# A two-part transformer on one core: wider token chunks, transform steps laid among attention steps, branch outputs kept in DRAM

## The chip, the core and the metric

The kernel runs on one core of a Trainium2 chip. The metric is the device time of one execution in microseconds (us). Engines: TensorE (PE) multiplies, VectorE (DVE) and ScalarE (ACT) do the element-wise work, GpSimd (POOL) a little, and SyncE (SP) issues all the DMAs from one queue, in order.

## The reference

Batch 1, 256 tokens, width 1024, all in fp32. The first part is a stack of two layers; each is a mixer, a cross-attention to 256 memory rows and a convolutional feed-forward net (FFN), with residual sums. The second part has two layers over a context stream and a token stream, which share weights:

```
x  = x + mixer(norm(x));  x = x + xattn(norm(x), norm(mem));  x = x + conv_ffn(norm(x))    # two layers
h  = modulate(x),  hc = modulate(xc);   proj = h @ w_in,  projc = hc @ w_in                # second part, two layers
o_mla  = attend(q_mla,  [k_mla_c,  k_mla_l],  [v_c, v_l])      # 8 heads, latent keys
o_gqa  = attend(q_gqa,  [k_gqa_c,  k_gqa_l],  [v_c, v_l])      # 8 heads, 2 key heads
o_four = real(fft over tokens and over the 128 columns of a group)   # 4 groups
y  = sig(g0)*(o_mla @ w0) + sig(g1)*(o_gqa @ w1) + sig(g2)*(o_four @ w2)
x  = x + gt1 * (y @ w_o);   x = x + gt2 * conv_ffn_2(modulate(x))
```

In the first of the second part's layers the context stream goes through all of this too; in the last layer only its keys and values are needed.

## The kernel before

**Products.** A weight matrix comes in units of 128 rows by up to 1024 columns. `Stream.unit` (L1501 and on) issues the DMA of one unit into a `raw` tile (five of them), ACT casts it to a high half (L106) and DVE takes the rest as a low half (L107); `hi` and `lo` have four buffers each. Each product is three fp32r matmuls, high by high, high by low and low by high: `mm3` (L127 to L129) has the weights stationary and gives features by tokens; `mm3t` (L133 to L135) has 128 tokens stationary and streams weight columns. `tok` calls `mm3t` chunk by chunk: normally 256 columns, both token halves in one PSUM bank; with `wide=True` 512 columns, a bank for each token half. Chunks of 512 columns were in use for the first half of each FFN's down product and in `mixer1`; all others were 256 wide.

**PSUM.** Eight banks: `mm` 2, `acc` 2, `at` 2 (logits), `tp` 1 (transposes), `ao` 1 (attention output). `use` says which of them the names A and B stand for.

**SBUF slots.** Activations of 2 KB a partition come from one pool of 25 slots, attention outputs, transform outputs, merge sums and their split halves among them.

**Order.** The program is written in an order by hand, and a planner then orders each engine's instructions by simulated time, with the written order as priority; a tile's buffer has to be free before its writer is placed. Independent work is written in as steps of generators: `fill` takes steps of the spare generator (the memory's keys and values, then the context stream's part of the second half), `tick` takes steps of the modulation product (L842 to L844). In the second part `layer2` walks the string `ORDER`: N norm of the tokens, K and V keys and values, G and Q queries, O one step of the grouped attention, A one of the latent attention (four each), F the whole transform, c, b and B steps of the context stream. After it `MERGE` says in which order the three gated branch sums (0 latent, 1 grouped, 2 transform) are written; each is a loop over 8 pairs of feature blocks.

**One attention step** (`attend`, L1166 and on) is, for two token halves: logits of two heads (L1178, into `at`), maximum on DVE (L1187), exponential on ACT (L1189), reciprocal and scaling on DVE (L1191, L1192), transposes (L1197, `tp`), copy on ACT (L1198), then weights times values (L1200, `ao`), and a copy to the slot `oa` (L1204).

**The transform** (`fourier`, L1208 and on) first loads three constants into `dr` tiles and splits them, once a layer. For each of 4 groups it then makes the features of all streams (`mm`), splits them, multiplies by the column transform (`acc`), splits, and multiplies by the token transform (`ao`).

## Time and profile before

| | us |
|---|---|
| median of 3 runs | 2317.23 (2313.97 to 2317.65) |
| the profiled execution's own time | 2314.78 |
| its span, first to last instruction | 2313.0 |
| PE busy | 2273.5 (98%) |
| DVE busy | 1510.2 (65%) |
| ACT busy | 1199.2 (52%) |
| DMA engines, mean busy share of the main queue | 48.1% |
| mean granted TensorE clock | 0.996 |

PE counts as busy while any matmul is under way. Matmuls overlap: one lasts longer than the step from its start to the next one's start, so a short wait between two can leave the busy time nearly whole. A row of the windows view has the stretch, its length, then for each engine its busy time and number of instructions (x) in the order PE, PEld (weight loads), DVE, ACT, POOL, then the granted clock (PEclk, 1.00 is 2.4 GHz), the busy share of the DMA engines and GB/s; for one line alone, only the engines that run it are there. In the timeline a row is start, duration, engine, line, operation, tiles and count. Stages by time: first layer 0 to 480 us, second layer 480 to 920, first layer of the second part 920 to 1820 (attention to 1140, merge sums to 1360, output and FFN after it), last layer 1820 to 2313 (attention to 2010).

### The profile page before, as it was taken

The numbers are of one execution on the slowest core, as the hardware profiler recorded it, in microseconds if no ns is written. First come the engines' busy times: TensorE is split into PE (matmuls) and PEld (weight loads), VectorE is DVE, ScalarE is ACT, GpSimd is POOL, SyncE is SP. The second block draws the span as 40 slices with busy tenths as digits, with TensorE's granted clock in tenths as the row PEclk, the third lists the DMA queues.
The fourth block names the chain that finished last, engine by engine and source line by source line (L and its number), as shares of the span: only waits on it lengthen the run. The fifth ranks groups of instructions, "written<-read, shape, count | busy, mean of one in ns | idle before, by whom it ended". The sixth has DMA issues, their size and how long they took to land.

```text
span 2313.0 us, 43514 instructions
## 1 busy us (share of the span) xinstructions
PE 2273.5 (98%) x17424; PEld 2104.5 (91%) x17424; DVE 1510.2 (65%) x2734; ACT 1199.2 (52%) x2220; POOL 106.6 (5%) x162
## 2 busy tenths in 40 slices
PE   8999999999999999899999999999999999999999
PEld 8899998988999999889899998789779989999999
DVE  6755586866757777776544446654566676677876
ACT  5655564654656555666433434331344566655554
POOL 2000000000001000121000000000000131000000
PEclk9999999999999999899999999999999999999999
DMA  8354576567446765323233244444444433375563
GB/s 274 122 171 147 180 245 220 172 199 264 130 133 215 236 195 177 114 65 102 65 120 121 92 164 147 155 157 130 166 158 142 144 115 128 102 243 177 173 201 128
DMA packets 114140, 369.29 MB, mean 160 GB/s; under 512 B 13432, under 2 KB 21505, under 8 KB 113937
## 3 DMA queue, kind: packets, MB, share of 16 engines
q1 hardware_dynamic: 113936, 366.50, 48.1%
q8 instruction: 137, 2.24, 0.4%
q14 instruction: 67, 0.54, 0.1%
HBM read 365.36 MB, written 1.09 MB: 158 GB/s over the span
## 4 chain that ended last, share of the span: by engine, by line
PE 94%; DVE 2%; ACT 2%; DMA 1%; issue 1%; POOL 0%; SPq 0%; POOLq 0%; ACTq 0%; DVEq 0%
PE mm L127 11%; PE mm L128 11%; PE mm L129 11%; PE acc L133 8%; PE acc L134 8%; PE acc L135 8%; PE acc L127 6%; PE acc L129 6%; PE acc L128 6%; PE at L1178 2%; PE ao L844 2%; PE mm L133 2%; PE mm L134 2%; PE mm L135 2%; PE ao L1200 2%; PE tp L1197 1%
## 5 line engine op out<-in xcount | busy, mean ns | idle before, releaser
L107 DVE TENSOR_TENSOR lo<-raw,hi 128x1024 fp32r<-128x1024 f32 (+4 forms) x615 | 709.6, 1158 | 447.9 <-ACT hi L106 437.9
L106 ACT CAST hi<-raw 128x1024 fp32r<-128x1024 f32 (+4 forms) x615 | 608.1, 994 | 666.5 <-PE mm L128 231.3
L127 PE MATMUL mm<-xt,hi 128*128 128x256 f32 (+1 forms) x1552 | 465.5, 300 | 2.1 <-ACT zq L961 2.0
L129 PE MATMUL mm<-xt,lo 128*128 128x256 f32 (+1 forms) x1552 | 461.4, 297 | 0.5 <-DVE lo L107 0.5
L128 PE MATMUL mm<-xt,hi 128*128 128x256 f32 x1376 | 391.7, 285 | 0.2 <-DVE xt L294 0.2
L127 PEld LDWEIGHTS mm<-xt,hi 128*128 128x128 f32 x1552 | 298.4, 192 | 22.3 <-issue 11.0
L129 PEld LDWEIGHTS mm<-xt,lo 128*128 128x128 f32 x1552 | 298.5, 192 | 8.6 <-DVE lo L107 1.1
L128 PEld LDWEIGHTS mm<-xt,hi 128*128 128x128 f32 x1376 | 265.4, 193 | 0.6 <-DVE xt L294 0.4
L129 PE MATMUL acc<-xt,lo 128*128 128x256 f32 (+1 forms) x704 | 218.4, 310 | 0.0
L127 PE MATMUL acc<-xt,hi 128*128 128x256 f32 (+1 forms) x704 | 217.9, 310 | 0.0
L128 PE MATMUL mm<-xc,hi 128*128 128x256 f32 (+1 forms) x544 | 174.1, 320 | 0.0
L128 PE MATMUL acc<-xt,hi 128*128 128x256 f32 x528 | 149.4, 283 | 0.0
L127 PEld LDWEIGHTS acc<-xt,hi 128*128 128x128 f32 x704 | 134.3, 191 | 7.8 <-issue 0.8
L129 PEld LDWEIGHTS acc<-xt,lo 128*128 128x128 f32 x704 | 134.3, 191 | 6.9
L133 PE MATMUL acc<-hi,wh 128*128 128x256 f32 x480 | 136.1, 285 | 0.0
L135 PE MATMUL acc<-hi,wl 128*128 128x256 f32 x480 | 135.8, 283 | 0.0
L134 PE MATMUL acc<-lo,wh 128*128 128x256 f32 x480 | 135.6, 283 | 0.0
L128 PEld LDWEIGHTS mm<-xc,hi 128*128 128x128 f32 x544 | 103.4, 190 | 7.7 <-DVE xc L294 0.3
L127 PE MATMUL mm<-xc,hi 128*128 128x256 f32 x368 | 105.1, 286 | 1.1 <-DVE xc L297 1.1
L129 PE MATMUL mm<-xc,lo 128*128 128x256 f32 x368 | 105.3, 286 | 0.0
L128 PEld LDWEIGHTS acc<-xt,hi 128*128 128x128 f32 x528 | 101.3, 192 | 0.1
L133 PEld LDWEIGHTS acc<-hi,wh 128*128 128x128 f32 x480 | 91.8, 192 | 3.0 <-issue 1.6
(489 smaller groups left out, 5167.1 us busy)
## 6 DMA issues: line engine op xcount, KB each, us to landing
raw<-in_w_up_dram SPq DMA_DIRECT2D x176, 512.0 KB, 3.6
raw<-in_w_mod_dram SPq DMA_DIRECT2D x96, 512.0 KB, 4.6
raw<-in_w_gb_dram SPq DMA_DIRECT2D x96, 512.0 KB, 3.6
raw<-in_w_dna_dram SPq DMA_DIRECT2D x30, 512.0 KB, 3.7
raw<-in_w_f_dram SPq DMA_DIRECT2D x25, 512.0 KB, 3.5
raw<-in_w_dnb_dram SPq DMA_DIRECT2D x24, 512.0 KB, 3.4
raw<-in_w_dn_dram SPq DMA_DIRECT2D x24, 512.0 KB, 3.7
raw<-in_w_qk_dram SPq DMA_DIRECT2D x16, 512.0 KB, 4.7
```

Source lines behind the costliest of these rows:

```text
L106: self.nc.scalar.copy(out=hi, in_=src)
L107: self.nc.vector.tensor_sub(out=lo, in0=src, in1=hi.bitcast(F32))
L127: m(ps, whi, xhi, start=first, stop=False)
L128: m(ps, whi, xlo, start=False, stop=False)
L129: m(ps, wlo, xhi, start=False, stop=last)
L133: m(ps, xhi, whi, start=first, stop=False)
L134: m(ps, xhi, wlo, start=False, stop=False)
L135: m(ps, xlo, whi, start=False, stop=last)
L844: nc.tensor.matmul(ps[32 * j:32 * j + 32, half * T:half * T + T], self.cs[:, k], raw[:, j], start=(k + half == 0), stop=(k + half == 8), t ...
L1178: lg = lambda u, i: nc.tensor.matmul(pss[i][:, u], qf(j, i, t), kf(j, i, u), start=True, stop=True)
L1197: nc.tensor.transpose(tp[:, u], es[(4 * g + u) // nk][:, u % nk], self.ident)
L1200: self.beside(nk, lambda u, i: nc.tensor.matmul(ops[64 * i:64 * i + 64, t], vf(j, i, u), pts[i][:, u], start=(u == 0), stop=(u == nk - 1)))
```

## The change

1. **512-column chunks.** The first two 256-column chunks become one of 512 in: the values of `mixer0` (chunks 2 and 3, `values2`), the four output projections of mixers and cross-attentions (`project`), the second half of both first-part FFNs, the second half of the second part's FFN for the context stream of its first layer and for the tokens of its last. The memory's values of layer 0 are two chunks of 512 instead of four of 256. They use the `mm` banks; their evictions handle one token half at a time.
2. **Orders.** The transform becomes a generator with one step a group, each merge sum one with 8 steps. In the first of the two layers the four F steps stand among the tokens' O and A steps; in the last layer they stand singly, and the 8 steps of branch sum 2 among the A steps. The context's steps (b) are spread over more places. Merge sums run in the order 1, 0, 2 and 2, 1, 0. In `kv_latent` the chunks run keys, values, keys, values. The transform's second product goes to `mm` instead of `ao`.
3. **Constants.** The transform's constants are loaded and split once, after the context is loaded, and stay.
4. **Branches by memory.** In the first of the two layers each pair of attention outputs, and each transform group, is written to DRAM (`put`, 12 writes of 256 KB), and each merge sum reads its branch back (`get`, 12 reads) into halves of `raw` tiles.
5. Slots 28 instead of 25; `FILL` and the list `dense` are fitted to the smaller number of steps; the first step of the spare generator (load and norm of the memory) moves from the seventh to the fourth place among `mixer0`'s dense steps.

```diff
-SLOTS, RAWS, SPLITS = 25, 5, 4
-ORDER = "NccccccccGQbbKBGVbVVVVOQbOOOQAAAA", "NccGQBGKVVQOFOVQVVOAAAOA"
+SLOTS, RAWS, SPLITS = 28, 5, 4
+ORDER = "NccccccccGQbbKbGbVbBOFOVOVOQFAVAVFQAFA", "NccGQBGKVVQOFOFVQOFVVOFA2A2A22A2222"
-MERGE = "10F2", "210"
-FILL = (1, 0, 1, 1, 2), (4, 0, 0, 1, 0), 0, (5, 0, 0, 0, 0), (5, 1, 0, 1, 0)
+FILL = (0, 1, 0, 1), (4, 0, 1, 0), 0, (5, 0, 0, 0), (5, 1, 1, 0)
...
-            self.tok(sv, 2 * c - 2, xt, 2, vout(c))
+            self.tok(sv, 0, xt, 2, vout(c))
+
+        def values2():
+
+            def f(t, ps):
+                for i in range(2):
+                    if not t:
+                        v[2 + i] = self.slot([P, 2, T], name="v")
+                        nc.scalar.activation(out=v[2 + i][:, 0], in_=ps[:, 0, T * i:T * i + T], func=AF.Identity, scale=r[:, 0:1])
+                    else:
+                        nc.vector.tensor_scalar(out=v[2 + i][:, 1], in0=ps[:, 0, T * i:T * i + T], scalar1=r[:, 1:2], scalar2=None, op0=ALU.mult)
+            self.tok(sv, 2, xt, 2, f, width=512, per=2, wide=True)
...
-        dense = [lambda: values(2), lambda: qpair(4), lambda: qpair(5), lambda: values(3), lambda: qpair(6), lambda: qpair(7)]
+        dense = [values2, lambda: qpair(4), lambda: qpair(5), lambda: self.fill(1), lambda: qpair(6), lambda: qpair(7)]
...
         st = self.stream(wname)
         self.fill(fill[0])
-        for c in range(4):
+        self.tok(st, 0, o, 2, self.add_half(0, True), width=512, per=2, wide=True, tag="mm")
+        self.fill(fill[1])
+        for c in (2, 3):
             self.tok(st, 2 * c, o, 2, self.add_res(c))
-            self.fill(fill[c + 1])
+            self.fill(fill[c])
...
-            for c in range(4):
+            self.tick(2)
+            self.tok(second, 0, hs, 2, self.add_half(0, True), width=512, per=2, wide=True, tag="mm")
+            for c in (2, 3):
                 self.tick()
-                last = l == 1 and js[-1] == 21 and c == 3
-                self.tok(down, 3 * c, hs, 2, self.add_res(c, job=job if last else None), last=last)
+                last = l == 1 and c == 3
+                self.tok(down, 3 * c - 6, hs, 2, self.add_res(c, job=job if last else None), last=last)
...
-        for c in range(4):
+        for c in (0, 2, 1, 3):
...
-        four = None
+        four = {}
         ss = (1,) if last else (0, 1)
-        xs = lambda: [L.x[s] for s in ss]
         merge = self.merge(L.l, ss)
+
+        def piece(o):
+
+            if o not in gs:
+                xs = [L.x[s] for s in ss]
+                gs[o] = self.fourier(self.stream(f"w_f{L.l}"), xs, ss, four) if o == "F" else merge(int(o), (L.om, L.og, four)[int(o)], xs)
+            return gs[o]
+
         for o in ORDER[last]:
             if o == "N":
                 self.norm1(L, 1)
             elif o == "K":
                 self.kv_grouped(L, 1)
-            elif o == "F":
-                four = self.fourier(self.stream(f"w_f{L.l}"), xs(), ss)
...
-                next(gs[o], None)
-        for o in MERGE[last]:
-            if o == "F":
-                four = self.fourier(self.stream(f"w_f{L.l}"), xs(), ss)
-            else:
-                merge(int(o), (L.om, L.og, four)[int(o)], xs())
+                next(piece(o), None)
+        for o in ("102", "10")[last]:
+            for _ in piece(o):
+                pass
...
-            out[s, j] = o[:, j % 2]
-            nc.scalar.copy(out=out[s, j], in_=ops.rearrange("p t q -> p (t q)"))
+            nc.scalar.copy(out=o[:, j % 2], in_=ops.rearrange("p t q -> p (t q)"))
+            if spill is None:
+                out[s, j] = o[:, j % 2]
+            elif j % 2:
+                d = self.put(f"{spill}{s}{j}", o.rearrange("p t q -> p (t q)"))
+                out[s, j - 1], out[s, j] = (d, 0), (d, 1)
             yield
 
-    def fourier(self, sf, xs, ss):
+    def dft_setup(self):
+
+        def const(w, name, tag):
+            raw = self.work([P, w], "dr")
+            self.nc.sync.dma_start(out=raw, in_=self.a[name] if w == T else self.a[name][int(tag[2])])
+            return raw
+
+        ts = [self.cp.tile([P, 1536], F32R, name="dft", tag=f"fm{t}") for t in range(2)]
+        cl = [Xt(t[:, :512], t[:, 512:1024]) for t in ts]
+        for t in range(2):
+            self.split(const(512, "dft_l", f"fm{t}"), cl[t].hi, cl[t].lo)
+        cc = Xt(ts[0][:, 1024:1280], ts[0][:, 1280:])
+        self.split(const(T, "dft_c", ""), cc.hi, cc.lo)
+        self.dft = cc, cl
...
+    def put(self, key, t):
+
+        d = self.dram.tile([P, 512], F32, name="br", tag=f"br{key}")
+        self.nc.sync.dma_start(out=d, in_=t)
+        return d
+
+    def get(self, branch):
+
+        ds = []
+        for d, _ in (v for v in branch.values() if isinstance(v, tuple)):
+            if not any(d is x for x in ds):
+                ds.append(d)
+        at = []
+        for n, d in enumerate(ds):
+            if n % 2 == 0:
+                raw = self.rawp.tile([P, 1024], F32, name="raw", tag="raw")
+            w = raw[:, 512 * (n % 2):512 * (n % 2) + 512]
+            self.nc.sync.dma_start(out=w, in_=d)
+            at.append(w)
+        view = lambda d, c: next(a for a, x in zip(at, ds) if x is d)[:, c * T:c * T + T]
+        return {k: view(*v) if isinstance(v, tuple) else v for k, v in branch.items()}
...
-        cc = self.wide(T)
-        raw = self.work([P, T], "dr")
-        nc.sync.dma_start(out=raw, in_=self.a["dft_c"])
-        self.split(raw, cc.hi, cc.lo)
-        cl = []
-        for t in range(2):
-            raw = self.work([P, 512], "dr")
-            nc.sync.dma_start(out=raw, in_=self.a["dft_l"][t])
-            c = self.wide()
-            self.split(raw, c.hi, c.lo)
-            cl.append(c)
-        out = {}
+        cc, cl = self.dft
         for g in range(4):
             ps = self.bank([P, W])
             self.feats(ps, sf, 5 + g, xs)
             x = self.wide(W)
             self.evac(ps, x)
-            op = self.bank([P, W], "ao")
+            op = self.bank([P, W])
...
             nc.scalar.copy(out=o, in_=op)
+            d = self.put(f"f{g}", o) if len(xs) > 1 else None
             for n, s in enumerate(ss):
-                out[s, g] = o[:, n * T:n * T + T]
-        return out
+                out[s, g] = o[:, n * T:n * T + T] if d is None else (d, n)
+            yield
...
-            o = []
+            o, branch = [], self.get(branch)
...
-            if last:
-                down = self.stream("w_dnb2", 3, 768)
-                for c in range(4):
-                    self.tok(down, 3 * c, hs, 2, self.gated(gt, c, ss, True, True, c == 3), last=c == 3)
-                continue
-            if base == 0:
+            if not base:
                 for c in range(4):
                     self.tick()
-                    self.tok(down, 6 * c, hs, 2 * ns, self.gated(gt, c, ss, False))
+                    self.tok(down, 3 * c, hs, 2 * ns, self.gated(gt, c, ss, False))
                 continue
             for s in ss:
-                for c in range(4):
+                x = hs if last else self.part(hs, s)
+                if last or not s:
+                    self.tick(2 - s)
+                    self.tok(self.stream(f"w_dnb2_{l}", 6, 512), 0, x, 2, self.gated_half(gt, 0, s, not last, last), width=512, per=2, wide=True, tag="mm")
+                down = self.stream(f"w_dnc2_{l}", 3, 768)
+                for c in ((2, 3) if last or not s else range(4)):
                     self.tick(s == 0 or c == 0)
-                    self.tok(self.stream(f"w_dn2_{l}", 3, 768), 6 * c + base, self.part(hs, s), 2, self.gated(gt, c, (s,), last=c == 3), last=c == 3)
-                if s == 0:
+                    self.tok(down, 3 * c if not last else 3 * c - 6, x, 2, self.gated(gt, c, (s,), True, last, c == 3), last=c == 3)
+                if s == 0 and not last:
```

## Rows read from the trace of the kernel before

**Rows 1.** page, part 1: busy us of each engine, share of the span, instructions
```profile
PE 2273.5 (98%) x17424; PEld 2104.5 (91%) x17424; DVE 1510.2 (65%) x2734; ACT 1199.2 (52%) x2220; POOL 106.6 (5%) x162
```

**Rows 2.** windows: busy time of each engine in six stretches
```profile
920.00:980.00 60.00, 54.01 (x406) 48.94 (x406) 47.18 (x123) 39.00 (x93) 9.46 (x9) 0.92 0.41 135
980.00:1060.00 80.00, 78.18 (x680) 70.81 (x679) 56.19 (x158) 55.28 (x142) 16.00 (x19) 0.97 0.24 75
1060.00:1140.00 80.00, 78.12 (x706) 70.68 (x706) 46.10 (x108) 45.90 (x100) 3.35 (x5) 1.00 0.20 62
1140.00:1360.00 220.00, 220.00 (x1614) 209.38 (x1614) 99.03 (x122) 78.10 (x110) 0.00 (x0) 1.00 0.36 116
...
1820.00:1860.00 40.00, 36.80 (x296) 35.55 (x295) 29.68 (x59) 23.11 (x54) 8.73 (x8) 1.00 0.42 129
1860.00:2010.00 150.00, 143.71 (x1254) 133.39 (x1252) 101.31 (x221) 99.34 (x215) 24.88 (x26) 0.99 0.33 107
```

**Rows 3.** timeline of PE, layer-2 tail, 256 columns, first and 36th: start, us, what
```profile
2289.73 0.28 PE L135 MATMUL acc<-hi,hl 128*128 128x256 f32 x1
...
2293.93 0.28 PE L134 MATMUL acc<-lo,hl 128*128 128x256 f32 x1
```

**Rows 4.** timeline of PE, first FFN, 512 columns, first and 32nd
```profile
804.84 0.39 PE L135 MATMUL acc<-hi,hb 128*128 128x512 f32 x1
...
811.86 0.39 PE L133 MATMUL mm<-hi,hb 128*128 128x512 f32 x1
```

**Rows 5.** timeline of PE, one attention step: starts that follow without a wait
```profile
1103.86 1.09 PE L1200 MATMUL ao<-pt,vm 128*64 128x128 f32 x16
1104.89 0.66 PE L1197 MATMUL tp<-ident,e 128*128 128x128 f32 x4
1105.38 1.06 PE L1178 MATMUL at<-kq 96*128 96x128 f32 x8
1106.19 0.36 PE L129 MATMUL mm<-xt,lo 128*128 128x256 f32 x1
```

**Rows 6.** timeline of PE, grouped logits and what follows
```profile
1046.40 1.71 PE L1178 MATMUL at<-kvg,qtg 64*128 64x128 f32 x16
1048.04 0.44 PE L133 MATMUL mm<-hi,hl 128*128 128x384 f32 x1
```

**Rows 7.** windows of line L1178 alone (logits) in both attention stretches
```profile
980.00:1140.00 160.00, 39.32 (x312) 34.67 (x312) 0.99 0.22 68
1860.00:2010.00 150.00, 32.73 (x256) 28.27 (x256) 0.99 0.33 107
```

**Rows 8.** the same for line L1197, the transposes
```profile
980.00:1140.00 160.00, 26.83 (x168) 18.20 (x168) 0.99 0.22 68
1860.00:2010.00 150.00, 18.88 (x120) 13.06 (x120) 0.99 0.33 107
```

**Rows 9.** the same for line L1200, values times weights
```profile
980.00:1140.00 160.00, 25.25 (x354) 18.73 (x356) 0.99 0.22 68
1860.00:2010.00 150.00, 15.33 (x226) 11.96 (x226) 0.99 0.33 107
```

**Rows 10.** windows of PE with and without fill, then the memory's norm
```profile
1060.00:1100.00 40.00, 39.58 (x373) 37.28 (x372) 23.80 (x61) 21.89 (x47) 3.35 (x5) 1.00 0.31 94
1100.00:1127.00 27.00, 25.96 (x256) 23.06 (x255) 14.37 (x34) 16.22 (x39) 0.00 (x0) 1.00 0.07 21
...
100.00:112.00 12.00, 9.06 (x75) 8.00 (x74) 11.75 (x52) 9.08 (x35) 1.44 (x2) 1.00 0.41 136
```

**Rows 11.** tile view of the transform's constants (dr)
```profile
L106 ACT CAST wh<-dr x4: 616/620/624, 1249.0 to 1909.1; 128x512 fp32r<-128x512 f32 x4
```

**Rows 12.** DMA issues: what, count, KB, median us to landing
```profile
gt<-gates SPq DMA_DIRECT2D x12, 256.0 KB, 3.8
...
out_dram<-x SPq DMA_DIRECT2D x3, 256.0 KB, 2.2
```

**Rows 13.** waits of SP's own queue: us in total, times, longest
```profile
SPq L1322 <- DVE x L1320: 21.8, 5, 7.5
```

More of the change, by code (lines that the diff above doesn't have):

```diff
@@ L355, in add_res, with add_half @@
         return f
-    def add_half(self, c):
+    def add_half(self, c, final=False):
         def f(t, ps):
@@ L361, in f @@
             self.nc.vector.tensor_add(out=d, in0=ps[:, 0], in1=d)
+            if final and t:
+                for i in (2 * c, 2 * c + 1):
+                    self.chunk(i)
+                    if self.last:
+                        self.last.chunk(i)
         return f
@@ L589, in vout @@
             v.append(s)
+        def vout(t, ps):
+            for i in range(2):
+                if not t:
+                    v.append(self.slot([P, 2, T], name="mv"))
+                nc.vector.tensor_copy(out=v[len(v) - 2 + i][:, t] if t else v[-1][:, t], in_=ps[:, 0, T * i:T * i + T])
         st = self.stream(f"w_mk{l}")
@@ L597, in mem_kv @@
         st = self.stream(f"w_mv{l}")
-        for c in range(4):
-            self.tok(st, 2 * c, xt, 2, vout)
+        for c in range(4 if l else 2):
+            if l:
+                self.tok(st, 2 * c, xt, 2, vout1)
+            else:
+                self.tok(st, 4 * c, xt, 2, vout, width=512, per=2, wide=True)
             yield
@@ L648, in ffn1 @@
         nc.sync.dma_start(out=cw, in_=self.a[f"conv{l}"])
-        up, first, down = self.stream(f"w_up{l}"), self.stream(f"w_dna{l}", 6, 512), self.stream(f"w_dnb{l}", 3, 768)
+        up, first, second, down = self.stream(f"w_up{l}"), self.stream(f"w_dna{l}", 6, 512), self.stream(f"w_dnb{l}", 6, 512), self.stream(f"w_dnc{l}", 3, 768)
         for js in (range(0, 11), range(11, 22)):
@@ L1208, in fourier @@
+    def fourier(self, sf, xs, ss, out):
         nc = self.nc
         W = len(xs) * T
-        cc = self.wide(T)
-        raw = self.work([P, T], "dr")
-        nc.sync.dma_start(out=raw, in_=self.a["dft_c"])
-        self.split(raw, cc.hi, cc.lo)
-        cl = []
-        for t in range(2):
-            raw = self.work([P, 512], "dr")
-            nc.sync.dma_start(out=raw, in_=self.a["dft_l"][t])
-            c = self.wide()
-            self.split(raw, c.hi, c.lo)
-            cl.append(c)
@@ L1329, in gated, with gated_half @@
         return f
-    def gated_half(self, gt, c):
+    def gated_half(self, gt, c, s=1, sums=False, final=False):
+        x, sm = ((self.xc if not s else None, getattr(self, "ssc", None)), (self.x, self.ss))[s]
         def f(t, ps):
             w = self.work([P, 512], "gr")
-            self.nc.vector.tensor_tensor(out=w, in0=ps[:, 0], in1=gt[1, c], op=ALU.mult)
-            d = self.x[:, t, 512 * c:512 * c + 512]
+            self.nc.vector.tensor_tensor(out=w, in0=ps[:, 0], in1=gt[s, c], op=ALU.mult)
+            d = x[:, t, 512 * c:512 * c + 512]
             self.nc.vector.tensor_add(out=d, in0=d, in1=w)
+            if final:
+                self.nc.sync.dma_start(out=self.out[0, t * P:t * P + P, 512 * c:512 * c + 512], in_=d)
+            elif sums:
+                for i in (2 * c, 2 * c + 1):
+                    self.sumsq(x, sm, i, (t,))
         return f
@@ L1531, in tmode, with first512, down @@
         return c(w.reshape(kt // per, per, P, n // width, width).transpose(3, 0, 2, 1, 4).reshape(-1, P, per * width))
-    def down(w, n=2):
+    def first512(w):
+        return np.concatenate([tmode(w[:, :512], 512, 2), tmode(w[:, 512:])])
+    def down(w, n):
         z = np.zeros((P, w.shape[1]), w.dtype)
-        if n == 2:
-            return tmode(np.concatenate([w[:11 * P], z, w[11 * P:], z]))
-        return tmode(np.concatenate([w[11 * P:], z])) if n else tmode(np.concatenate([w[:11 * P], z]), 512, 2)
+        w = np.concatenate([w[11 * P:] if n in (1, 2, 4) else w[:11 * P], z])
+        return (tmode(w, 512, 2), tmode(w[:, :512], 512, 2), tmode(w[:, 512:]), tmode(w), tmode(w))[n]
     def cols(v):
@@ L1567, in lay @@
         r[f"w_mk{l}"] = fmode(f("xattn_wkv")[l][:, :D])
-        r[f"w_mv{l}"] = tmode(f("xattn_wkv")[l][:, D:])
-        r[f"w_xo{l}"] = tmode(f("xattn_wo")[l])
+        r[f"w_mv{l}"] = tmode(f("xattn_wkv")[l][:, D:], *((512, 2), ())[l])
+        r[f"w_xo{l}"] = first512(f("xattn_wo")[l])
         r[f"w_up{l}"] = pairs(f("ffn_w_up")[l])
-        r[f"w_dna{l}"], r[f"w_dnb{l}"] = (down(f("ffn_w_down")[l], n) for n in range(2))
+        r[f"w_dna{l}"], r[f"w_dnb{l}"], r[f"w_dnc{l}"] = (down(f("ffn_w_down")[l], n) for n in range(3))
         r[f"conv{l}"] = convs(f("ffn_conv_w")[l], f("ffn_conv_b")[l])
@@ L1604, in lay @@
         r[f"w_up2_{l}"] = pairs(f("w_up_2")[l])
-        if l:
-            r["w_dna2"], r["w_dnb2"] = (down(f("w_down_2")[l], n) for n in range(2))
-        else:
-            r["w_dn2_0"] = down(f("w_down_2")[l])
+        r["w_dna2" if l else "w_dn2_0"] = down(f("w_down_2")[l], 0 if l else 3)
+        r[f"w_dnb2_{l}"], r[f"w_dnc2_{l}"] = (down(f("w_down_2")[l], n) for n in (1, 2 if l else 4))
         r[f"conv2_{l}"] = convs(f("conv_w_2")[l], f("conv_b_2")[l]).reshape(P, NF, 2, 4)
```

17 lines of the change are left out of this document (9 added, 8 removed).

## The prediction

> **What bounds the kernel now.** I read the page's first part, then stretches of the span, then the starts of single matmuls. The page has PE busy for 98% of the span, DVE for 65, ACT for 52 [rows 1]: PE is the bound, and the time is the sum of what its matmuls take plus what it waits. Busy time hides most of the waits, since a 256-column matmul is written down as 0.28 us while the next one starts 0.12 us after it [rows 3]; so I count from start to start. In a dense run that step is (2293.93 - 2289.73)/35 = 0.120 us at 256 columns [rows 3] and (811.86 - 804.84)/31 = 0.2265 us at 512 [rows 4].
>
> The windows then show where PE does not run at that pace. From 1140 to 1360 us, the merge sums with the whole transform among them, it is busy for all of 220 us: nothing is to be had there [rows 2]. The two attention stages differ: it is idle for 6.0 us of 920 to 980, for 1.8 and 1.9 us of the next two stretches, for 3.2 us of 1820 to 1860 and 6.3 us of 1860 to 2010, and the granted clock falls to 0.92 and 0.97 in the first two, so part of the time PE runs at 1.2 GHz instead of 2.4 [rows 2].
>
> How much is lost there in all I count by kind. In one attention step that does not wait, 16 matmuls of values times weights take 1.03 us to the next start, four transposes 0.49, eight latent logits 0.81 [rows 5], sixteen grouped logits 1.64 [rows 6]: 0.064, 0.122 and twice 0.102 us each. From 980 to 1140 us there are 312 logits, 168 transposes and 354 of the values [rows 7 to 9], and 1386 - 834 = 552 others [rows 2]: 31.8 + 20.5 + 22.7 + 552 x 0.12 = 141.2 us of work in 160, a loss of 18.8. From 1860 to 2010 the same with 256, 120, 226 and 652: 26.1 + 14.6 + 14.5 + 78.2 = 133.4 of 150, a loss of 16.6. Some of the others are wider than 256 columns, so these are upper ends, 35 us together; the lower ends are the idle times, 3.7 and 6.3, together 10 us.
>
> **The change part by part.** The sum is made against the profiled execution, 2314.8 us; the median of the three runs is 2.4 us above it, and I add that at the end.
>
> *512-column chunks.* Each pair of 256-column matmuls becomes one. Pairs: `mixer0`'s values 8 feature blocks x 2 token halves x 3 = 48; four projections of 48, 192; the memory's values twice 48, 96; the first part's two FFNs 11 x 2 x 3 = 66 each, 132; the second part's two layers 66 each, 132. That is 600 pairs, and each saves 2 x 0.120 - 0.2265 = 0.0135 us: -8.1 us, all on PE, hence on the path. Weight bytes, splits and evictions keep their amounts. The bounds are 0 and -8.1: what could take it back is the `mm` banks, a rival below.
>
> The Trainium skill, "TensorE: Matmul & The Clock Gate", section "Back-to-back issue gap", gives an isolated step as N/2.4 + 2.5 ns: 109 ns at 256 columns and 216 at 512, so a pair would save 2.6 ns and the 600 pairs 1.6 us, not 8.1. The rows differ: the fixed part here is 0.0135 us a matmul, five times as much [rows 3, 4], and the measurement decides.
>
> *Orders in the first attention stage.* The string has the same first fourteen letters, so the start of the stage up to about 980 us, where the tokens' normed features are only just made, has nothing new that could run: 0, with bounds of -3 and +3, half its idle time either way. After it the four transform steps come among O, V and A. They bring their own matmuls from the merge stretch, which ran without a loss, so moving them costs nothing in itself; what they can win is the loss of 980 to 1140.
>
> *Orders in the last layer.* Here the transform stood among the attention already; what is new is that it comes in single steps, and that the 8 steps of branch sum 2 follow the A steps one by one. The win can come from 1860 to 2010; before it (1820 to 1860) the order is the same and I take 0.
>
> How much of a loss goes with more to fill in? Between 1060 and 1100 us the planner had laid gate products of the merge between the attention steps, and PE was idle for 0.42 of 40 us, 1.05%; from 1100 to 1127 there were none left and it was idle for 1.04 of 27, 3.85% [rows 10]. So fill takes away 0.73 of it. Of the lower ends that is 7.3 us, of the upper ones 25.6; I take the middle, -16.4 us for both stages. The ends are 0 (the fill only trades places with what the planner lays there already) and -35.
>
> *Constants.* Three splits and loads less in the last layer's stage, and in the first they go to an earlier place; a 512-wide cast is 0.62 us on ACT [rows 11]. ACT is busy for 99 of those 150 us and DVE for 101 [rows 2]: off the path, 0, within the bounds of the stage.
>
> *Branches by memory.* Twelve writes and twelve reads of 256 KB. Nearest rows: a 256 KB load lands 3.8 us after its issue, a 256 KB store 2.2 [rows 12]. The transfers lie beside a stage whose DMA engines are busy for 0.20 to 0.36 [rows 2]. The reads are at the head of branch sums whose first matmuls are gate products that don't need them. What counts is SP's queue: a write stands in it until ACT has copied the branch output, and the weight loads behind it stand too. The nearest row is the final stores, which held the queue 5 times for 21.8 us, 4.4 each [rows 13]. Weights are loaded up to five units ahead, and one unit feeds 24 matmuls of 0.12 us, 2.9 us; so two loaded units cover such a hold, and I cost it at 0. With no cover it is 12 x 4.4 = 53 us.
>
> *Memory's norm.* It stalled PE from 100 to 112 us: 2.9 us idle while DVE was busy for 11.75 of 12 [rows 10]. It now stands three steps earlier, among the same softmax work of DVE; 0, with -3 and +3.
>
> Sum: 2314.8 - 8.1 - 16.4 = 2290.3, plus 2.4: **2293 us**.
>
> **The rivals.**
>
> *Only the chunks pay.* The waits in the attention are chains through DVE and ACT, and the planner reaches ahead in the written order already, as the gate products at 1060 us show. Then the transform's steps only push others out: 2317.2 - 8.1 = 2309. For it speaks that 980 to 1060 lost as much idle time as 1060 to 1140 [rows 2]; against it the difference in rows 10.
>
> *More goes than I take.* Both stages lose all 35 us and the starts of the stages half of their 9.2 us idle [rows 2], because with 28 slots and without the constants' five slots the transform's features can run ahead of the places where they are written: 2317.2 - 8.1 - 35 - 4.6 = 2269.
>
> *The branch writes hold up the weights (slower).* Place: SP's queue in the first attention stage. If a write waits for its copy when the loaded units are used up, PE waits too. It decides from an uncovered hold of 24.5/12 = 2.0 us a write on; with the row's 4.4 us uncovered the time is 2293 + 53 = 2346, with 3 us 2329. The Trainium skill, "DMA: Bandwidth & Descriptors", section "Anatomy of one DMA — SWDGE (gpsimd) path", states that a DMA's semaphore wait happens on the issuing sequencer before dispatch, which is this rival's mechanism; the SP waits of rows 13 agree with it. Against it: the weights' own loads mostly wait for a free buffer, so the queue runs ahead.
>
> *The banks give the chunks back.* A 512-column chunk takes both `mm` banks, where its forerunner took `acc`. At the end of `mixer1` the transposes of the last heads sit in `mm`, and the first k blocks, up to 36 matmuls or 4.3 us, can no longer run ahead of them. At 1 us in each of eight places the 8.1 us are gone; with the attention unchanged too that is 2317, no change.
>
> **How the numbers follow.** The forecast has 0.50, its own range 2282 to 2303. Only the chunks: 0.18. More goes: 0.16. The writes: 0.10. The banks, with nothing won: 0.06. About 0.2%, 4.6 us, can be told from no change. Faster by more than that: 0.50 + 0.16 + 0.14 of the chunks' 0.18 = 0.80. Within it: 0.04 + 0.05 of the banks = 0.09. Slower: 0.10 + 0.01 = 0.11. The range goes from 2270, close to the second rival, to 2316.
>
> **What would show it.** Right: 512-column rows at 0.227 us from start to start in the projections and FFNs, 600 of them in the place of 1200 of 256 columns; transform products (`acc`, then `mm`) between the exponentials of both attention stages, with PE idle under 2% of them; a merge stretch in the first layer shorter by the transform's time, with PE busy throughout; SP waits on the branch writes that no PE wait follows. Wrong: PE waits that end on a weight load or its split right after a write (the third rival), an attention stage that grew by as much as the merge shrank (the first), PE waits at the first matmul of a 512 chunk (the fourth).

## The result and the profile after

The changed kernel takes 2333.09 us (median of 4 runs, 2330.57 to 2333.57) against 2316.14 us before (median of 4, 2313.97 to 2317.65): ratio 1.0072, 95% interval 1.0054 to 1.0089, so 17 us slower. Its profiled execution took 2333.57 us, of which the span is 2331.8.

The page's first part after, to hold against [rows 1]:
```profile
PE 2283.3 (98%) x16824; PEld 2086.8 (89%) x16824; DVE 1511.0 (65%) x2735; ACT 1200.7 (51%) x2217; POOL 105.1 (5%) x162
```
There are 600 matmuls fewer, as worked out, and 512 columns still take 0.226 us a step, (613.07 - 606.73)/28, in a projection where nothing waits (timeline of PE in the projection after `mixer1`: start, us, what):
```profile
606.73 0.39 PE L133 MATMUL mm<-lo,s 128*128 128x512 f32 x1
...
613.07 0.39 PE L134 MATMUL mm<-hi,s 128*128 128x512 f32 x1
```
So PE has 8 us less to do, and the time rose all the same: PE lost 26 us more than before. (Loss, here and below, is the sum of steps from start to start less what the same matmuls take at the paces of [rows 3 to 6]; it is worked out for each 40 us of a trace.) The projections and the first attention stage carry most of it.

*The projections.* Timeline of PE at the end of `mixer1`, with idle time and what ended it in brackets:
```profile
591.11 0.28 PE L134 MATMUL acc<-hi,xc 128*128 128x256 f32 x1
591.23 0.60 PE L836 MATMUL mm<-ident,mh 128*128 128x128 f32 x4
595.49 6.55 PE L280 MATMUL mm<-diag,xc 128*128 128x128 f32 x32 [3.66 <-DVE diag L267]
602.33 0.47 PE L132 MATMUL mm<-hi,s 128*128 128x512 f32 x1 [0.29 <-DVE ev L291]
```
The projection's first 512-column matmul (L132) starts only behind 3.7 us of waiting and 32 matmuls of the context's norm (L280). Windows of both kernels over that place and over the second cross-attention's end (engines' busy time, then granted clock, DMA share, GB/s), before:
```profile
586.00:604.00 18.00, 18.00 (x149) 17.84 (x149) 13.11 (x24) 11.43 (x30) 1.84 (x4) 1.00 0.46 149
686.00:704.00 18.00, 18.00 (x147) 17.76 (x147) 9.89 (x16) 11.80 (x25) 0.70 (x1) 1.00 0.47 142
```
and after:
```profile
586.00:604.00 18.00, 14.05 (x89) 13.23 (x88) 13.25 (x28) 10.72 (x32) 1.44 (x3) 0.81 0.30 98
686.00:704.00 18.00, 14.99 (x72) 12.53 (x71) 8.70 (x18) 8.10 (x17) 3.44 (x5) 0.81 0.34 108
```
PE was busy throughout before; after it idles 4.0 and 3.0 us, and with each wait the clock falls from 2.4 GHz to 1.2 (granted clock 0.50 from 594.14 to 600.97 us and from 696.54 to 703.37; 0.81 as a mean of the 18 us). Together the two places lose 12 to 13 us more.

*The first attention stage.* The tokens' norm that opens it and the context's norm that closes the merge lie in these groups (all instructions of the norm's line by tile; "first start to last start"), before:
```profile
L1441 PE MATMUL at<-diag,x x64: 270/275/377, 919.7 to 2119.5; 128*128 128x128 f32 x64
L1441 PE MATMUL at<-diag,xc x32: 273/275/276, 1400.0 to 1786.2; 128*128 128x128 f32 x32
```
and after:
```profile
L1512 PE MATMUL at<-diag,x x64: 270/275/557, 926.5 to 2138.5; 128*128 128x128 f32 x64
L1512 PE MATMUL at<-diag,xc x32: 273/275/275, 1417.7 to 1804.7; 128*128 128x128 f32 x32
```
From the one to the other it took 1400.0 - 919.7 = 480.3 us and now 491.2. Windows after, to hold against [rows 2, 10]; the first layer's stage, its merge sums, the last layer's stage, the memory's norm, a stretch of the attention:
```profile
927.00:987.00 60.00, 55.92 (x393) 50.31 (x391) 44.94 (x116) 38.89 (x89) 9.04 (x9) 0.91 0.43 134
987.00:1172.00 185.00, 175.32 (x1552) 160.51 (x1552) 110.62 (x278) 107.04 (x255) 19.77 (x24) 0.99 0.22 72
1172.00:1360.00 188.00, 188.00 (x1327) 177.01 (x1326) 86.42 (x102) 66.82 (x90) 0.00 (x0) 1.00 0.43 141
...
1867.00:2017.00 150.00, 146.06 (x1248) 135.90 (x1247) 101.59 (x219) 97.65 (x212) 29.47 (x31) 0.99 0.34 106
100.00:112.00 12.00, 12.00 (x102) 11.04 (x101) 8.58 (x28) 6.78 (x22) 1.40 (x2) 1.00 0.33 110
1100.00:1140.00 40.00, 37.77 (x345) 35.90 (x344) 20.62 (x43) 23.04 (x48) 4.31 (x6) 1.00 0.25 85
```
With the transform in it, the stage from 987 to 1172 has PE idle for 9.7 of 185 us (5.2%), against 3.7 of 160 before; the merge, already free of loss, gave the transform away. The stretch from 1100 on is idle for 5.6%, more than what [rows 10] show for their stretch from 1100 on (3.85%). What PE waits for there (waits of PE from 987 to 1172: total, times, longest):
```profile
PE at L1209 <- ACT e L1220: 3.0, 4, 1.5
PE acc L132 <- ACT wh L298: 2.6, 2, 2.2
PE ao L1231 <- ACT pt L1229: 2.5, 4, 0.8
```
are the exponentials (L1220) and copies (L1229) that it waited for before, and as a new wait the split of the transform's own features (L298). The same view of the kernel before, from 980 to 1140:
```profile
PE ao L1200 <- ACT pt L1198: 1.7, 4, 0.7
PE at L1178 <- ACT e L1189: 0.7, 1, 0.7
```
SP's queue in that stage, gate weights, branch writes and reads alone (w_gb, br<-, raw<-br):
```profile
1076.39 0.33 SPq L1260 DMA_DIRECT2D br<-oa  x1
1083.00 12.42 SPq L1274 DMA_DIRECT2D raw<-br  x3
1105.82 0.32 SPq L1260 DMA_DIRECT2D br<-oa  x1
1106.70 0.32 SPq L1260 DMA_DIRECT2D br<-of  x1
1108.09 0.32 SPq L1274 DMA_DIRECT2D raw<-br  x1
1108.79 4.17 SPq L1580 DMA_DIRECT2D raw<-in_w_gb_dram  x2
```
The first gate weight of the merge is loaded at 1108.8 us, behind two writes and the fourth read; the first of these writes (1105.82) had held the queue for 10.3 us, until ACT had copied the attention output. Before, nine of them were loaded from 1033 us on, and gate products filled the attention (the same view of the kernel before):
```profile
1033.32 28.18 SPq L1509 DMA_DIRECT2D raw<-in_w_gb_dram  x9
```
In the last layer PE idles 3.9 of 150 us against 6.3, yet its loss from 1800 to 2040 stays at 23.0 us (23.2). The memory's norm, moved, no longer stalls (12.00 us busy of 12), and the first 200 us lose 8.7 us against 10.9.

### The profile page after: what moved, and what is told of

It reads as the page before. It is cut to its first block, busy times and chain, and to the rows that moved or that the text cites. A ratio compares the mean times of both kernels' runs of the same rounds, so it can differ in the third digit from the quotient of the medians.

```text
span 2331.8 us, 42344 instructions
## 1 busy us (share of the span) xinstructions
PE 2283.3 (98%) x16824; PEld 2086.8 (89%) x16824; DVE 1511.0 (65%) x2735; ACT 1200.7 (51%) x2217; POOL 105.1 (5%) x162
## 4 chain that ended last, share of the span: by engine, by line
PE 93%; ACT 2%; DVE 2%; DMA 2%; issue 1%; SPq 0%; POOL 0%; POOLq 0%; ACTq 0%; DVEq 0%
PE mm L126 11%; PE mm L128 11%; PE mm L127 11%; PE acc L132 6%; PE acc L126 6%; PE acc L128 6%; PE acc L127 6%; PE acc L133 6%; PE acc L134 6%; PE mm L132 3%; PE mm L133 3%; PE mm L134 3%; PE at L1209 3%; PE ao L872 2%; PE ao L1231 2%; PE tp L1228 2%
## 5 line engine op out<-in xcount | busy, mean ns | idle before, releaser
L132 PE MATMUL acc<-hi,wh 128*128 128x256 f32 x436 | 123.8, 285 | 0.0
L134 PE MATMUL acc<-hi,wl 128*128 128x256 f32 x436 | 123.4, 283 | 0.0
L133 PE MATMUL acc<-lo,wh 128*128 128x256 f32 x436 | 123.4, 283 | 0.0
L132 PEld LDWEIGHTS acc<-hi,wh 128*128 128x128 f32 x436 | 83.5, 192 | 3.0 <-issue 1.6
```

The costliest lines, as they stand in the source:

```text
L132: m(ps, xhi, whi, start=first, stop=False)
L133: m(ps, xhi, wlo, start=False, stop=False)
L134: m(ps, xlo, whi, start=False, stop=last)
```

## Experiments

All are timed in five rounds against the kernel before (2315 to 2316 us). "+" is the median's distance to it in the same rounds; the intervals reach 2 to 3 us either way. The ratio is worked out from all runs, so it can differ from the medians' distance by up to 2 us.

**The changed kernel with one word changed** (e1):
```diff
-        self.tok(st, 0, o, 2, self.add_half(0, True), width=512, per=2, wide=True, tag="mm")
+        self.tok(st, 0, o, 2, self.add_half(0, True), width=512, per=2, wide=True, tag="acc")
```


> The changed kernel with one word changed: the projections' 512-column chunk takes the two acc banks, not the two mm banks. Theory 'banks' (at the output projections of mixer1 and of the second cross-attention the 512 chunk stands in mm behind the context's norm and latents, PE waits and falls to half clock; 6 us lost at each): 2321, with the projections at 560-600 and 680-720 us back under 1 us of loss. Rival 'constants' (the transform's constants are split ahead of the context's norm and that alone delays it): the wait at 592 us stays, 2330 to 2333. Rival 'orders alone': within 2 us of 2333.


2331.9 us, ratio 1.0064 (1.0051 to 1.0076). The waits at 592 and 692 us are gone (loss of 560 to 600 down from 6.4 to 0.5 us, of 680 to 720 from 6.9 to 2.1), so 'constants' is out; but the time fell by 1 us only, which is what the rival 'orders alone' gave (the next two runs rule that one out). Part of it stands again at the projections' ends, the rest is scattered.

**The chunks alone, in mm and in acc** (e2, e3): the changed kernel with
```diff
-SLOTS = 28; ORDER = "NccccccccGQbbKbGbVbBOFOVOVOQFAVAVFQAFA", "NccGQBGKVVQOFOFVQOFVVOFA2A2A22A2222"
+SLOTS = 25; ORDER = "NccccccccGQbbKBGVbVVVVOQbOOOQAAAA", "NccGQBGKVVQOFOVQVVOAAAOA"; MERGE = "10F2", "210"
...
```
Branch outputs in SBUF and constants made in `fourier` as before; e3 has the projections' chunk in acc, as e1.


> The kernel before with the 512-column chunks alone (and the fill counts that belong to them); orders, branches in SBUF, 25 slots and constants as before. Theory 'banks': -8 for the chunks, +12.5 at the two projections: 2320, slower than before by 4. Rival 'constants': the two projections lose nothing, 2308. Rival 'more lost by the chunks elsewhere too' (the loss at the end of the first FFN): 2325 or more.

> As the chunks alone, with the projections' 512-column chunk in acc. Theory 'banks': 2308, the whole 8 us of the chunks. Rivals: if the chunks lose elsewhere, 2312 or more.


2328.2 us (1.0051, 1.0039 to 1.0064) and 2321.6 (1.0025, 1.0014 to 1.0035): the chunks alone make the kernel slower, by +11.9, and the bank is 6.5 us of that, half of what 'banks' said.

**Which chunks** (f1: the projections alone, f2: values and memory's values with the memory's norm moved, f3: the FFNs), each added to the kernel before (f1 and f2 with `FILL` fitted to their steps):
```diff
f1 -    for c in range(4): self.tok(st, 2 * c, o, 2, self.add_res(c))
f1 +    self.tok(st, 0, o, 2, self.add_half(0, True), width=512, per=2, wide=True, tag="mm")   # then c = 2, 3
f2 +    self.tok(sv, 2, xt, 2, f, width=512, per=2, wide=True)
f2 +    self.tok(st, 4 * c, xt, 2, vout, width=512, per=2, wide=True)
f3 +    self.tok(second, 0, hs, 2, self.add_half(0, True), width=512, per=2, wide=True, tag="mm")
```


> The kernel before with the 512-column chunk in the four output projections alone, in mm (192 pairs, 2.6 us less work). Theory 'banks': this part alone carries the loss of the chunks, so 2316 - 2.6 + 12 = 2326, with PE waits at the context's norm (590 us) and at its latents (690 us). Rival 'the order as written was fitted to its lengths' (any change of a chunk shifts what the planner lays, and each of the three parts loses some): 2320 here.

> The kernel before with the 512-column chunks in mixer0's values and the memory's values alone, with their fill counts (the memory's norm three steps earlier): 144 pairs, 1.9 us less work, and the 2 us that the norm's stall lost. Theory 'banks': no context work stands in mm there, 2312. Rival 'fitted to its lengths': 2318 to 2320.

> The kernel before with the 512-column chunks in the four FFNs alone: 264 pairs, 3.6 us less work. Theory 'banks': 2313, with at most 1 us back at the chunk after the last h block. Rival 'fitted to its lengths': 2318 to 2320.


f1 2334.3 us, +18.1 (1.0074, 1.0062 to 1.0086); f2 2315.8 (0.9992, 0.9983 to 1.0002); f3 2315.7 (0.9997, 0.9988 to 1.0007). The projections alone carry the loss, more than I expected: from 560 to 760 us f1 loses 17.5 us where the kernel before loses 2.7. Its longest wait there is the one above (waits of PE in f1, 590 to 632 us):
```profile
PE mm L281 <- DVE diag L268: 3.7, 1, 3.7
```

**All chunks but the projections'** (k4: f2 and f3 together).


> The 512-column chunks in values, memory values and FFNs together, none in the projections: 408 pairs, 5.5 us less work, and the memory's norm moved. If each keeps what it saves: 2309. By the two single measurements (-0.4 and -0.5): 2315.


2310.1 us, ratio 0.9972 (0.9961 to 0.9983): -5.7, what 408 pairs at 0.0135 us make (5.5). The agreement is in part luck: the memory's norm, moved, wins some 2 us more, which in the profiled execution are lost again elsewhere. This is the best kernel of the study, faster than both. With f1 it adds up to the chunks alone: 18.1 - 5.7 = 12.4, measured 11.9. That f2 and f3 one by one showed 0.4 and 0.5 is not explained: f2's interval (-3.9 to +0.5) still holds the 2 to 4 us that it should have won, f3's (-2.8 to +1.6) doesn't hold its 3.6. A single case shows how large the scatter is. Windows from 100 to 120 us of the kernel before and of f3, whose PE runs the same 1527 matmuls in the same order over the first 200 us:
```profile
100.00:120.00 20.00, 17.06 (x142) 15.99 (x141) 15.29 (x58) 12.93 (x44) 2.14 (x3) 1.00 0.26 83
```
```profile
100.00:120.00 20.00, 17.40 (x124) 16.28 (x123) 13.06 (x57) 11.60 (x42) 2.14 (x3) 0.83 0.22 72
```
The same waits let the clock fall in one execution (0.83) and not in the other, 2.3 us of difference.

**Bank or fill** (h2 and h1, both on f1):
```diff
h2 -FILL = ..., (5, 0, 0, 0), (5, 1, 1, 0)
h2 +FILL = ..., (4, 1, 0, 0), (2, 4, 1, 0)     # the context's norm, and three steps, behind the 512 chunk
h1 tag="acc", as in e1
```


> The chunks in the four projections alone (2334), with the context's work moved behind the 512 chunk: one step (the context's norm) after it in mixer1, three steps after it in the second cross-attention. Theory 'banks' (the chunk waits in mm behind those steps): the waits at 590 and 690 us go, 2316 to 2320. Rival 'less to run ahead' (a 512 chunk gives PE less to do before the last operand is there, whatever stands in mm): 2330 or more.

> The 512-column chunk in the four projections alone (2334 in mm), here in acc. By the step from mm to acc in the kernel with all chunks (-6.5): 2327. Theory 'banks' in full (nothing but the bank makes the loss): 2314. Rival 'less to run ahead': 2325 or more, with the waits moved to the end of the projections, at the transposes of the last chunk.


2333.2 us (1.0077, 1.0064 to 1.0090) and 2329.4 (1.0051, 1.0038 to 1.0064). Neither gives the old time back. In h2 the wait in the second cross-attention didn't go (last row below, 3.0 us idle and a clock of 0.91). The front of `mixer1`'s projection is clean (18.00 of 18.00 us busy), and the waits stand at its end, 4.8 us of the 28 (windows of h2; the kernel before was busy for 27.21 of the second):
```profile
586.00:604.00 18.00, 18.00 (x117) 16.49 (x116) 10.87 (x20) 7.71 (x14) 0.79 (x2) 1.00 0.37 124
604.00:632.00 28.00, 23.20 (x177) 21.74 (x177) 22.55 (x42) 20.92 (x55) 1.76 (x12) 1.00 0.44 143
686.00:704.00 18.00, 14.96 (x85) 12.69 (x84) 7.55 (x12) 8.31 (x21) 0.00 (x0) 0.91 0.25 74
```
Before, the planner wove the context's steps (mm) and the projection's chunks (acc) into each other, and each covered the other's waits (timeline of PE in the kernel before; what is left out are the projection's matmuls in acc and the last heads' transposes):
```profile
595.94 0.28 PE L133 MATMUL acc<-hi,s 128*128 128x256 f32 x1
...
602.73 1.95 PE L281 MATMUL mm<-diag,xc 128*128 128x128 f32 x16
...
607.15 1.05 PE L281 MATMUL mm<-diag,xc 128*128 128x128 f32 x8
```
With the chunk in mm they stand in line; with the steps moved behind, the end has a chain through DVE (`diag`, `ev`) that nothing covers; in acc (h1) the front is clean too, and the end idles 2.2 us of 28 and the second cross-attention's end 1.9 of 31. So the bank is 5 of the 18 us; the rest stays with the chunk in acc too. The chunk gives its result in one lump where there were two, and the planner lays everything around it anew; how much is the one and how much the other isn't settled.

**The orders without the chunks** (f4), and the changed kernel with the first layer's old order (e4: ORDER's first string as before, F in the merge, its last product in mm):


> The kernel before with everything of the change but the chunks: both orders, branches by memory, 28 slots, constants, the context's values step. If the parts add up (changed kernel 2333 less the chunks' +12): 2321, with the loss in the first attention stage. My prediction's own term was -16.4: 2300. Rival 'the two parts spoil each other' (the orders were good for the old chunks): 2316 or less.

> The changed kernel with the first layer's order of before (the transform stands in the merge stretch again); branches by memory, 28 slots, constants and the last layer's order as changed. Theory 'orders' (PE runs in a fixed order and waits for the transform's splits on ACT among the attention's exponentials; 11 us): 2322. Rival 'branch writes and reads' (they cost the 11 us): 2333, since they stay; the waits in 980-1160 us stay too.


f4 2332.4 us, +16.2 (1.0063, 1.0050 to 1.0075); e4 2334.0 (1.0076, 1.0063 to 1.0090). The terms that I had at -16.4 in all (orders -16.4, constants and branches 0) are +16.2. e4 refutes that the first string alone makes it: with the old string the time stays (the attention loses less, and the transform in the merge now loses 7.5 us from 1240 to 1320, where it lost none before).

**Apart** (on f4): g2 the old first string, F in the merge with its product in ao; g3 the same with F only put before the last four A; g4 the new string less its F.
```diff
g2 +ORDER[0] = "NccccccccGQbbKBGVbVVVVOQbOOOQAAAA"            then 1, 0, F, 2
g3 +ORDER[0] = "NccccccccGQbbKBGVbVVVVOQbOOOQAFAFAFAF"        then 1, 0, 2
g4 +ORDER[0] = "NccccccccGQbbKbGbVbBOOVOVOQAVAVQAA"           then 1, 0, F, 2
```


> The orders without the chunks (2332), but the first layer's order as before, its transform in the merge stretch and its last product in ao again; branches by memory, 28 slots, constants and the last layer's new order stay. Theory 'steps among the attention' (the rearranged first stage loses the 16 us): 2316 to 2318. Rival 'branch writes and reads' (SP's queue and the raw buffers): 2325 or more, since all twelve writes and reads stay.

> The orders without the chunks, with the first layer's order of before but for the transform's four steps, put one by one before the last four latent attention steps. If the transform's own steps cost the time (each holds mm and acc for its chain of copies and splits on ACT): 2328 to 2332. If the other shifts of the string cost it (context steps spread, latent values and queries later): 2316 to 2320. My prediction's mechanism (transform products fill the waits of the last steps): 2310.

> The orders without the chunks, with the first layer's new string less its four transform steps, which stand in the merge stretch as before (product in ao). If the other shifts of the string cost the time: 2328 to 2332. If the transform's steps do: 2316 to 2320.


g2 2328.3 us, +13.0 (1.0057, 1.0044 to 1.0069); g3 2326.3, +11.0 (1.0043, 1.0030 to 1.0057); g4 2337.4, +22.1 (1.0097, 1.0083 to 1.0110). So 13 us come with no transform step among the attention at all, and the other shifts of the string cost 9 more (g4 against g2). With the F steps among the attention 6 us come back in the new string and 2, within the noise, in the old one, but not because the steps fill anything. What goes is a loss of the transform in the merge. Windows of that place, g4 and f4:
```profile
1240.00:1310.00 70.00, 66.29 (x500) 63.34 (x499) 24.74 (x33) 21.38 (x35) 0.00 (x0) 0.98 0.21 72
```
```profile
1240.00:1310.00 70.00, 70.00 (x496) 65.95 (x496) 34.64 (x43) 24.95 (x34) 0.00 (x0) 1.00 0.43 143
```
From 1270 to 1320 us g4 loses 6.9 us and f4 0.1, g2 6.0 and g3 0.1. In the attention, the 240 us from the tokens' norm on, f4 loses 0.4 us more than g4, and g3 2.4 more than g2. In g2 the loss has two places that the kernel before doesn't have: 1040 to 1080 us (8.3 against 3.1) and the transform in the merge, 1280 to 1300 (6.1 against 0.1).

**Writes or reads.** Branch writes on ACT's queue, in the changed kernel (k1) and in g2 (k2); then g2 without writes and reads (m1):
```diff
k1, k2 -        self.nc.sync.dma_start(out=d, in_=t)
k1, k2 +        self.nc.scalar.dma_start(out=d, in_=t)
m1 -            d = self.put(f"f{g}", o) if len(xs) > 1 else None      m1 +  d = None
m1 -            ..., None if L.l else "m")                             m1 +  ..., None)     # "g" alike
```


> The changed kernel with the branch writes issued on ACT's queue, right behind the copy that they write, in place of SP's. Theory 'writes hold the weights' (in the changed kernel SP's queue stood 69 us behind the branch copies between 985 and 1190 us, with weight loads behind them): some 5 to 10 us of the first stage's loss go, 2324 to 2328. Rival 'steps among the attention' (PE waits for the chain of exponentials and splits itself): 2331 to 2333.

> The first layer's old order with branches by memory (2328), the writes on ACT's queue. Theory 'writes hold the weights': the 6.1 us lost at 1283 to 1296, where SP stood 34.5 us behind one write of the transform, go, and 2 to 4 us in 1040 to 1080: 2318 to 2320. Rival 'reads and raw buffers' (the reads take two of the five raw buffers): 2327.

> The first layer's old order, constants set up early, 28 slots, the last layer's new order (2328 with branches by memory, on SP's writes as on ACT's), here with every branch output kept in SBUF: no write, no read. Theory 'reads hold the gate weights' (a read stands on SP's queue until its write is done, and the gate weights of that branch sum are queued behind it: the first gate weight was loaded at 1070 us, in the kernel before at 1033): gate weights from about 1033 us on again, the 6 us at 1283 to 1296 and the 5 us at 1040 to 1080 go, 2316 to 2318. Rival 'constants, slots and last order': 2326 to 2329, no change.


k1 2333.3 us (1.0074, 1.0061 to 1.0087), k2 2330.1 (1.0057, 1.0044 to 1.0069): moving the writes alone wins nothing. m1 2321.1 us, +4.8 (1.0023, 1.0014 to 1.0032): writes and reads together are some 8 of the 13. SP's timeline from 1028 to 1074 us says how. k2:
```profile
1035.47 0.33 SPq L1544 DMA_DIRECT2D raw<-in_w_uq_dram  x1
1037.80 33.58 SPq L1245 DMA_DIRECT2D raw<-br  x3
1071.48 1.33 SPq L1544 DMA_DIRECT2D raw<-in_w_gb_dram  x3
```
m1:
```profile
1031.34 0.33 SPq L1544 DMA_DIRECT2D raw<-in_w_uq_dram  x1
1033.66 28.96 SPq L1544 DMA_DIRECT2D raw<-in_w_gb_dram  x9
```
In k2 three reads hold SP's queue for 33.6 us; the gate weights of that branch sum are queued behind. In m1 the queue takes nine gate weights in that time. In g2 it is the write that holds the queue. The longest waits of SP from 1030 to 1073 us, g2 and k2:
```profile
SPq L1231 <- ACT oa L1205: 30.1, 2, 29.5
```
```profile
SPq L1245 <- DMA br<-oa: 32.8, 2, 32.3
```
On SP's queue the write waits 29.5 us until ACT has copied the attention output; with the write on ACT's queue the read behind it waits 32.3 us until the write is done. So k1 and k2 don't show that the writes are free, only that the read then stands where the write stood. Reads on another queue, or later in the order, weren't tried. In m1 the loss of 1280 to 1300 goes too. The windows of 1050 to 1090 and 1240 to 1310, g2:
```profile
1050.00:1090.00 40.00, 37.83 (x333) 32.94 (x332) 29.43 (x77) 25.82 (x55) 5.12 (x8) 1.00 0.37 132
1240.00:1310.00 70.00, 65.75 (x505) 62.69 (x505) 26.63 (x37) 23.23 (x38) 0.00 (x0) 1.00 0.29 101
```
and m1:
```profile
1050.00:1090.00 40.00, 39.64 (x335) 35.81 (x334) 27.02 (x69) 24.60 (x49) 5.29 (x8) 1.00 0.44 132
1240.00:1310.00 70.00, 70.00 (x556) 68.50 (x556) 26.01 (x36) 23.22 (x38) 0.00 (x0) 1.00 0.23 75
```
Of the 8 us some 6 lie at 1280 to 1300, in the transform's stretch of the merge; of the 5 us expected at 1040 to 1080 only 2 went. The changed kernel doesn't have the first of these places (188.00 of 188.00 us busy from 1172 to 1360), so what writes and reads cost there was not measured. The remaining 4.8 us (28 slots, constants early, the chunk order in `kv_latent`, the last layer's order) weren't taken apart.

**What has paid, put together** (n3): k4 with the transform's steps before the last four A of the old string, every branch in SBUF, the last layer's old order (and the new chunk order in `kv_latent`).
```diff
+ORDER = "NccccccccGQbbKBGVbVVVVOQbOOOQAFAFAFAF", "NccGQBGKVVQOFFFFOVQVVOAAAOA"     # on k4; SLOTS = 28, dft_setup, no put
```


> What has paid, put together: the 512-column chunks everywhere but in the projections (2310), all branch outputs in SBUF, the last layer's order of before, and the transform's four steps before the last four latent attention steps of the first layer (28 slots, constants set up early). If transform products are a better fill than the gate products that stand there already (my prediction's mechanism, freed of the reads): 2300 to 2308. If they only take the gate products' place: 2310 to 2312. If the transform's own chain of copies and splits adds to ACT's work there: 2314 or more.


2319.3 us (1.0015, 1.0006 to 1.0024), 9 us slower than k4. From 1060 to 1150 us PE is busy for 85.64 of 90 us, in k4 for 88.12; the longest waits there (waits of PE in n3):
```profile
PE acc L132 <- ACT wh L298: 1.7, 2, 1.5
PE ao L1229 <- ACT pt L1227: 1.5, 2, 0.7
```
The first is PE at the transform's own second product, waiting for the split of its features: the step brings a chain through ACT of its own. In the 240 us from the tokens' norm on n3 loses 6.8 us more than k4. The 28 slots, the early constants and the order in `kv_latent` are in that too: m1, which has them and no transform there, loses 3.7 us more there than the kernel before. So the steps' own share of the 9 us isn't measured; that they win nothing there is.

## Why the prediction was wrong

The sum was -24.5 us (2293), and +17 came (2333). Three of its terms failed.

*Chunks, -8.1.* The term had 0 as its upper bound, and that bound failed. Outside the projections they pay what was worked out (-5.7 for -5.5, in part by luck). In the projections 192 pairs, -2.6 by the sum, are +18.1. The fourth rival had the place, the end of `mixer1`, and the shape, a wait ahead of the first 512-column matmul, but at 1 us a place; it was 3.7 us of waiting and the clock behind it. I looked at the transposes in mm and missed what the fill puts into the same banks there, the context's norm (L280) and latents. The bank is 5 of the 18 us; why the rest is lost stays open. (By the isolated step that the prediction quotes a pair saves 2.5 ns and 600 pairs 1.5 us, not 2.6 and 1.6; nothing hangs on it.)

*Orders in the first attention stage and the last layer's, -16.4.* The step that failed is "so moving them costs nothing in itself; what they can win is the loss of 980 to 1140". The transform's steps win nothing there in any pair of runs (f4 against g4, g3 against g2, n3 against k4). "Fill takes away 0.73 of it" was read from [rows 10], and the fill of those rows was gate products. The change put them off (gate weights from 1109 us on, not 1033) and put in their place steps with a chain of copies on ACT. The string's other shifts, 9 us of loss without the chunks (g4 against g2), had no term in the sum at all; by what mechanism they cost that is open. The bounds 0 to -35 excluded a loss, for no reason that the rows gave. In the last layer the loss stayed as it was.

The reading of [rows 10] was off as well: from 1100 us on there still is a part of a gate product, as the last line of [rows 5] shows; the last of it starts at 1107.35. Cut there, the windows of before are
```profile
1060.00:1107.60 47.60, 47.18 (x445) 44.58 (x444) 26.24 (x67) 24.48 (x54) 3.35 (x5) 1.00 0.26 80
1107.60:1127.00 19.40, 18.36 (x185) 15.76 (x183) 11.93 (x28) 13.64 (x33) 0.00 (x0) 1.00 0.09 28
```
PE is idle for 0.9% with fill and 5.4% without, so gate products took away 0.84 of the idle time, not 0.73. That makes the forecast's term larger, and the miss with it.

*Branches by memory, 0.* The step that failed is "the reads are at the head of branch sums whose first matmuls are gate products that don't need them". The products don't, but their weights stand on the same queue behind the writes and the reads. The third rival had queue and mechanism right; its hold was mis-sized. I took 4.4 us from the final stores, which two loaded units (5.8 us) cover; a hold here is 29.5 us in g2, and up to 21.6 in the changed kernel (SP at L1260, from 1145 to 1167 us). The price, some 8 us, is measured with the old string alone. The sentence of the Trainium skill that stood beside it ("DMA: Bandwidth & Descriptors", "Anatomy of one DMA — SWDGE (gpsimd) path": a DMA's semaphore wait happens on the issuing sequencer) agrees with the 29.5 us that SP stood at a write in g2 and the 32.3 at a read in k2.

*Constants, 0.* Not measured alone: they are in the 4.8 us of m1.

*Memory's norm, 0 (±3).* Within its bounds: some 2 us less over the first 200 us, in k4 (8.2) as in the changed kernel (8.7 against 10.9).

*The sum.* Chunks alone +11.9 and orders alone +16.2 make +28, the changed kernel has +17. The slices that don't add up are mostly those where the clock fell in each of the kernels: 920 to 1000 us (loss 16.9 before, 21.0 in e2, 19.9 in f4, 16.7 changed), 1400 and 2120 us, and the memory's norm, which f4 keeps. That they can't be lost twice is my reading, not shown.

## What to carry to other kernels

Before a tile moves to another pool or a transfer to another queue, list what the order already runs through that pool and queue at that place: a fill that covers a wait should share as little of them as it can with the work that it covers. A transfer that waits for a late producer, write or read, holds up everything queued behind it, even what the next step could begin with. And a stretch that is full because of its fill says nothing on what another fill would do there.

## What was not expected of the hardware

The clock turned out a price on top of waits: with the wait of 3.7 us at 592 us, and again with one of 2.1 us at 693 us behind two of 0.4 and 0.6, PE ran at 1.2 GHz for 6.8 us (mean granted clock 0.81 over 18 us). Over the whole span the mean granted clock is 0.992 after and 0.996 before. From these, as an estimate, PE stood at 1.2 GHz for some 37 us and some 18, so at most some 9 of the 26 us that it lost more (half of the difference) are the clock's. And it is not the same from run to run: with the same matmuls in the same order it read 0.83 in one profiled execution and 1.00 in another.
